# Which engine computes the low halves of the expert weights: VectorE and GpSimd by turns, or VectorE alone

## The chip, the cores and the metric

The kernel runs on one core of a Trainium2 chip. A core has TensorE (PE: matmuls, with its weight loads shown apart as PEld), VectorE (DVE), ScalarE (ACT), GpSimd (POOL) and SyncE (SP, which here issues the weight loads). The engines run side by side, each in its own order, and wait for one another through semaphores. The metric is the time of one execution in microseconds (us), as the median over several.

## The reference

Two blocks are run one after the other on 256 tokens of width 1024. The first has two layers of feed-forward, a convolution and recurrence mixer, and feed-forward again. The second has modulation, a recurrence beside an attention with selected keys, and at its end a mixture of 16 experts, the only part that the change touches:

```
y = zeros
for e in 16 experts:
    he = silu(hf @ w1[e]) * (hf @ w3[e])          # 1024 -> 512
    y = y + combine[:, e:e+1] * (he @ w2[e])      # 512 -> 1024
x = x + g2 * y
```

Each token has one group of four experts, and two experts within it; `combine` is zero for the others. All data are fp32.

## The kernel before, in words

**Weights in halves.** All weights lie in DRAM as blocks of 128 x 2048 numbers (1 MB), in the order of use. A block is two halves of 128 x 1024. A half has to be split before TensorE can use it: ScalarE writes its rounded copy (L197, type fp32r, the high half), and then VectorE or GpSimd subtracts that from the original (L202, the low half). A product is then three matmuls: high by high, weight low by input high, weight high by input low. For each weight half the experts do 6 matmuls of 512 columns.

**What sets the order.** `Weights.pump` issues the split of the next half: one cast on ScalarE, one subtraction on VectorE or GpSimd. It does so only while fewer than 6 halves (`NSPLIT`) are split or being split and not yet used up. `done` is called after the matmuls of a half: it frees that half's buffer, pumps one more, and lets background work take a step. So in the experts ScalarE and VectorE run some 6 halves ahead of TensorE, and each engine works strictly in the order written. SyncE loads blocks into 5 raw buffers, in the experts 2 more (`spare`); a raw buffer comes free when both of its halves are split.

**Which engine subtracts.** `W.gp` decides in L198: with 0 all subtractions go to VectorE, with n every n-th half goes to GpSimd. Elsewhere in the program it has the values 0, 1 and 2. Ahead of the experts it is 1 (five halves are split on GpSimd in advance); L1666 sets 3 for the experts.

**The experts.** The tokens of a group are gathered by a matmul with a 0/1 matrix (`gather`, L1511) and turned (`turn_gathered`, tile xg). For expert e, `up(e)` does 4 halves of w1 (m1) and 4 of w3 (m3) into the PSUM tile hp (L1536). VectorE then forms he (`weighted`, L1560). One expert later `turn(e)` transposes he on TensorE (L947), and VectorE and ScalarE split the result into ht (L317, L318). `down(e-1)` follows `up(e)`: 4 halves of w2 into y (L1594; for the last expert L1581). After each group `scatter` scales y (L1603), splits it (yh, L317, L318), multiplies it back to the tokens (L1612, L1613) and adds it to xres (L1614); its pieces are steps between the halves of the next but one expert. In the first expert a background job computes the routing weights in some 25 tiny VectorE instructions (L1458 to L1477), and `turn(0)` stands after the second half of w3 of expert 1.

Of the kernel before, what the change touches and what calls it, by code (L numbers as in the profile page):

```python
# [230 lines left out]
def kernel(ctx, tc, x, blocks, vecs, lnrows, consts, rows, bias_w, wr, out):  # L231
# [7 lines left out]
    W = Weights(tc, blocks, order, raw_pool, split_pool)  # L239
# [36 lines left out]
            soon.popleft()()  # L276
        step(M_WORK if work is None else work)

    # ---------------------------------------------------------------- start
    xres = apool.tile([128, 2, 1024], F32, name="xres")  # L280
    ident = cpool.tile([128, 128], F32, name="ident")
    vec = cpool.tile([128, NV], F32, name="vec")
# [96 lines left out]
    def new_xT():  # L379
        return apool.tile([128, 2, 8, 256], F32R, tag="xT", name="xT")  # L380
# [413 lines left out]
             lambda T, new: to_xT(xn, xres[:, T], T, new), xn, [("e1", l, 1, q) for q in range(4)])  # L794
        return xn

    # ------------------------------------------------------------ constants
    def setup():
        z = p1.tile([128, 6, 16], F32, name="sp")
        zv = [z[:, i] for i in range(6)]  # L800
        for l in range(2):
            nc.vector.tensor_scalar(z[:, 0, 8 * l:8 * l + 8], vec[:, l * V_LAYER + V_AP:l * V_LAYER + V_AP + 8],
                                    -1.0, None, op0=ALU.mult)
        nc.scalar.activation(zv[1], zv[0], AF.Abs)
        nc.scalar.activation(zv[1], zv[1], AF.Exp, scale=-1.0)
        nc.vector.tensor_scalar(zv[2], zv[1], 2.0, None, op0=ALU.add)
        nc.vector.reciprocal(zv[2], zv[2])
        nc.vector.tensor_mul(zv[1], zv[1], zv[2])
        nc.vector.tensor_mul(zv[2], zv[1], zv[1])
        n = 9  # L810
        nc.vector.tensor_scalar(zv[3], zv[2], 1.0 / (2 * n + 1), 1.0 / (2 * n - 1), op0=ALU.mult, op1=ALU.add)
        yield 0.6
        for k in range(n - 2, -1, -1):
            nc.vector.tensor_mul(zv[3], zv[3], zv[2])
            nc.vector.tensor_scalar(zv[3], zv[3], 1.0 / (2 * k + 1), None, op0=ALU.add)
        yield 1.2
        nc.vector.tensor_mul(zv[3], zv[3], zv[1])
        nc.vector.tensor_scalar(zv[0], zv[0], 0.0, None, op0=ALU.max)
        nc.vector.scalar_tensor_tensor(zv[3], zv[3], 2.0, zv[0], op0=ALU.mult, op1=ALU.add)
        for l in range(2):  # L820
            nc.vector.tensor_scalar(lruc[:, l, 0], z[:, 3, 8 * l:8 * l + 8], -8.0, None, op0=ALU.mult)
            nc.vector.tensor_scalar(lruc[:, l, 1], z[:, 3, 8 * l:8 * l + 8], 8.0, None, op0=ALU.mult)
        yield 0.5
# [44 lines left out]
                            ext_s[0:8, None, :].to_broadcast([8, 128, 512]))  # L868
        yield 0.1

    # ----------------------------------------------------------- the blocks
    xT = new_xT()
    to_xT(xT, xres[:, 0], 0, mid=lambda: W.pump(1))()
    W.pump(1)
# [9 lines left out]
                xT = ffn(l, part // 2, xT, l == 1 and part == 2)  # L884
    s1.close()

    # --------------------------------------------------------- second block
    s2 = ExitStack()
    p2 = s2.enter_context(tc.tile_pool(name="p2", bufs=1, reuse_waits="tile"))

# [442 lines left out]
    turn_[1] = True  # L1333
    s2.close()

    # ------------------------------------------------------- mixture of experts
    s3 = ExitStack()
    p3 = s3.enter_context(tc.tile_pool(name="p3", bufs=1, reuse_waits="tile"))
    g1b = p3.tile([128, 1024], F32, tag="yg", bufs=2, name="g1b")
# [323 lines left out]
    def early():  # L1663
        bg.append(weigh())

    W.gp = 3  # L1666
    experts(W, early, late)

    flag = nc.values_load(over[0:1, 0:1], min_val=0, max_val=1)
    with tc.If(flag > 0):  # L1670
# [4 lines left out]
        W = W2  # L1675
# [132 lines left out]
```

## Time and profile before

| | before |
|---|---|
| median of 3 runs (lowest to highest) | 1862.24 us (1861.23 to 1865.07) |
| span of the profiled execution | 1862.0 us |
| PE busy | 1755.7 us, 94% |
| DVE busy | 1328.0 us, 71% |
| ACT busy | 975.1 us, 52% |
| POOL busy | 547.4 us, 29% |
| L202 on DVE (raw) | 444 of 1510 ns, 663.1 us |
| L202 on POOL (raw) | 167 of 2655 ns, 442.1 us |

Busy time is an average over very different stages. The experts' matmuls start at 1528.3 us from the start of the span and end with it. In that stage the question is which engine the others wait for, so the stage has to be cut into stretches, and each read by itself. All positions below are us from the start of the span.

### The profile page before, as it was taken

The page shows a single profiled execution, that of the slowest core. Times are in us where ns is not written, and L with a number is a line of the kernel's source. Part 1 is how long each engine was busy: PE and PEld are TensorE (multiplying, and loading weights), DVE is VectorE, ACT ScalarE, POOL GpSimd, SP SyncE. Part 2 cuts the span into 40 slices and gives each one's busy share as a digit, 9 for nine tenths or more (in the row PEclk, how much of TensorE's full clock was granted, in tenths as well). Part 3 has the DMA queues.
Part 4 walks back from the last instruction along what each step waited for, and adds up shares of the span by engine and source line. Part 5 has one row for each costly group of instructions (what it writes and reads, how often), then busy time and mean ns, then how long its engine had stood idle before and what let it go on. Part 6 is the DMA issues. An engine that isn't in the chain of part 4 may idle for free. (4 is left out here: it accounts for less than half of the span.)

```text
span 1862.0 us, 27925 instructions
## 1 busy us (share of the span) xinstructions
PE 1755.7 (94%) x11369; PEld 1588.3 (85%) x11369; DVE 1328.0 (71%) x1569; ACT 975.1 (52%) x1340; POOL 547.4 (29%) x257
## 2 busy tenths in 40 slices
PE   8789999999999999999999999999798988999997
PEld 7789899999899989998989988999697666877775
DVE  6276778855756675668787466555878567899997
ACT  5254465654544444444756444444456456776773
POOL 0000144353200020003434441000546344555552
PEclk9989999999999999999999999999899889999999
DMA  7676554555556665765545646555333257978882
GB/s 291 170 261 253 219 181 159 182 205 180 216 203 241 248 246 181 255 242 204 182 159 186 211 147 243 190 181 181 129 113 108 108 230 268 348 283 335 302 315 115
DMA packets 57256, 394.26 MB, mean 212 GB/s; under 512 B 6912, under 2 KB 7216, under 8 KB 10912
## 3 DMA queue, kind: packets, MB, share of 16 engines
q1 hardware_dynamic: 52416, 375.94, 55.4%
q0 software_dynamic: 4128, 15.72, 3.0%
q8 instruction: 91, 1.49, 0.3%
q10 hardware_dynamic: 576, 0.74, 0.1%
q14 instruction: 45, 0.37, 0.1%
HBM read 389.20 MB, written 3.17 MB: 211 GB/s over the span
## 5 line engine op out<-in xcount | busy, mean ns | idle before, releaser
L202 DVE TENSOR_TENSOR split<-raw,split 128x1024 fp32r<-128x1024 f32 x444 | 663.1, 1510 | 293.1 <-ACT split L197 289.8
L202 POOL TENSOR_TENSOR split<-raw,split 128x1024 fp32r<-128x1024 f32 x167 | 442.1, 2655 | 1101.0 <-ACT split L197 1089.0
L197 ACT CAST split<-raw 128x1024 fp32r<-128x1024 f32 x611 | 628.4, 1048 | 256.1 <-PE mm L325 64.4
L323 PE MATMUL mmo<-xT,split 128*128 128x256 f32 x1248 | 354.0, 284 | 0.0
L324 PE MATMUL mmo<-xT,split 128*128 128x256 f32 x1248 | 353.7, 283 | 0.0
L325 PE MATMUL mmo<-xT,split 128*128 128x256 f32 x1248 | 353.6, 283 | 0.0
L325 PE MATMUL mm<-xT,split 128*128 128x256 f32 x968 | 274.2, 283 | 2.4 <-POOL split L202 2.4
L323 PE MATMUL mm<-xT,split 128*128 128x256 f32 x968 | 274.1, 283 | 0.0
L324 PE MATMUL mm<-xT,split 128*128 128x256 f32 x968 | 274.0, 283 | 0.0
L323 PEld LDWEIGHTS mmo<-xT,split 128*128 128x128 f32 x1248 | 239.4, 192 | 1.7
L324 PEld LDWEIGHTS mmo<-xT,split 128*128 128x128 f32 x1248 | 239.3, 192 | 1.7
L325 PEld LDWEIGHTS mmo<-xT,split 128*128 128x128 f32 x1248 | 239.3, 192 | 0.0
L376 PE MATMUL acc<-split,ht 128*128 128x512 f32 x816 | 200.6, 395 | 15.7 <-ACT split L197 15.5
L1536 PE MATMUL hp<-split,xg 128*128 128x512 f32 x768 | 190.6, 401 | 2.2 <-DVE split L202 1.4
L376 PEld LDWEIGHTS acc<-split,ht 128*128 128x128 f32 x816 | 150.3, 190 | 46.0 <-ACT split L197 15.7
L325 PEld LDWEIGHTS mm<-xT,split 128*128 128x128 f32 x968 | 185.3, 191 | 2.8 <-POOL split L202 2.8
L323 PEld LDWEIGHTS mm<-xT,split 128*128 128x128 f32 x968 | 185.3, 191 | 1.3
L324 PEld LDWEIGHTS mm<-xT,split 128*128 128x128 f32 x968 | 185.3, 191 | 1.3
L1536 PEld LDWEIGHTS hp<-split,xg 128*128 128x128 f32 x768 | 143.6, 190 | 38.3 <-DVE split L202 3.9
L1594 PE MATMUL y<-split,ht 128*128 128x512 f32 x360 | 89.8, 402 | 4.8 <-DVE ht L318 4.8
L1594 PEld LDWEIGHTS y<-split,ht 128*128 128x128 f32 x360 | 67.4, 190 | 22.8 <-DVE ht L318 7.4
L202 DVE TENSOR_TENSOR split<-spare,split 128x1024 fp32r<-128x1024 f32 x37 | 69.8, 1915 | 9.0 <-ACT split L197 9.0
(455 smaller groups left out, 2335.6 us busy)
## 6 DMA issues: line engine op xcount, KB each, us to landing
raw<-in_w_dram SPq DMA_DIRECT2D x328, 1024.0 KB, 4.9
spare<-in_w_dram SPq DMA_DIRECT2D x27, 1024.0 KB, 5.6
lng<-in_ln_dram POOLq DMA_DIRECT2D x6, 1024.0 KB, 4.9
raw<-in_w_dram SPq DMA_DIRECT2D x4, 512.0 KB, 7.6
scr<-ext_s POOLq DMA_DIRECT2D x1, 2048.0 KB, 47.4
cb<-in_row_dram POOLq DMA_DIRECT2D x3, 512.0 KB, 5.5
norm<-mrow POOLq DMA_DIRECT2D x2, 512.0 KB, 4.7
braw<-scr POOLq DMA_DIRECT2D x2, 512.0 KB, 4.8
```

The lines of the kernel that those rows point to most:

```text
L197: self.nc.scalar.copy(t[:, 0], r)
L202: eng.tensor_sub(t[:, 1], r, t[:, 0].bitcast(F32))
L323: nc.tensor.matmul(ps, w[:, 0, k], xT[:, 0, k], start=(k == 0), stop=False)
L324: nc.tensor.matmul(ps, w[:, 0, k], xT[:, 1, k], start=False, stop=False)
L325: nc.tensor.matmul(ps, w[:, 1, k], xT[:, 0, k], start=False, stop=(k == 7))
L376: nc.tensor.matmul(acc[T][n], a[:, hx], half[:, hw, n * 512:n * 512 + 512], start=(first and hx == 0 and hw == 0), stop=(last and hx == 1))
L1536: nc.tensor.matmul(ps, xgs[g][:, hx, k], wv[:, hw, kk], start=(k == 0 and hx == 0 and hw == 0), stop=(k == 7 and hx == 1))
L1594: nc.tensor.matmul(ys[g][n][:, 0:w], ht[:, hx, q], half[:, hw, o:o + w], start=(j == 0 and q == 0 and hx == 0 and hw == 0), stop=(j == 3 a ...
```

## The change

One number is changed: for the experts `W.gp` is 0 and no longer 3. Five comment lines are also made empty, which issues nothing and keeps the line numbers.

```
     def early():
         bg.append(weigh())

-    W.gp = 3
+    W.gp = 0
     experts(W, early, late)
```

On GpSimd's list, all that stood between the five subtractions ahead of the experts and the end goes. Before (h2s is the input of the experts, L1669 reads a flag after them):

```order
L1441 TENSOR_TENSOR h2s<-hh,h2s 128x1024
L202 TENSOR_TENSOR split<-raw,split 128x1024 x6
L202 TENSOR_TENSOR split<-spare,split 128x1024
L202 TENSOR_TENSOR split<-raw,split 128x1024 x4
...
L202 TENSOR_TENSOR split<-raw,split 128x1024 x4
L1669 TENSOR_LOAD over
```

And now:

```order
L1441 TENSOR_TENSOR h2s<-hh,h2s 128x1024
L202 TENSOR_TENSOR split<-raw,split 128x1024 x5
L1669 TENSOR_LOAD over
L1670 COMPARE_AND_BRANCH
```

62 subtractions leave GpSimd. The lists of TensorE and of ScalarE are the same as before.

On VectorE they stand where their halves come in the order. At the start of the experts, from the last routing numbers (cb) to the first he and ht, the list was:

```order
L1477 TENSOR_TENSOR cb<-rt 128x8
L202 TENSOR_TENSOR split<-spare,split 128x1024 x2
L202 TENSOR_TENSOR split<-raw,split 128x1024 x3
L1560 SCALAR_TENSOR_TENSOR he<-hp,cs,sl 128x512
L1488 TENSOR_REDUCE rt<-rank 128x1
L1489 TENSOR_SCALAR over<-rt 128x1
L1434 TENSOR_SCALAR Ps<-kc_14206,pos 128x128 x6
L202 TENSOR_TENSOR split<-raw,split 128x1024 x2
L318 TENSOR_TENSOR ht<-mm,ht 128x512
```

and is now:

```order
L1477 TENSOR_TENSOR cb<-rt 128x8
L202 TENSOR_TENSOR split<-spare,split 128x1024 x2
L202 TENSOR_TENSOR split<-raw,split 128x1024 x5
L1560 SCALAR_TENSOR_TENSOR he<-hp,cs,sl 128x512
L1488 TENSOR_REDUCE rt<-rank 128x1
L1489 TENSOR_SCALAR over<-rt 128x1
L1434 TENSOR_SCALAR Ps<-kc_14206,pos 128x128 x6
L202 TENSOR_TENSOR split<-raw,split 128x1024 x3
L318 TENSOR_TENSOR ht<-mm,ht 128x512
```

Ahead of the first he stand two subtractions more, and one more between it and the first ht.

Later, in the first scatter, VectorE's list between two he was this (ygs, yh and xres are the scatter's):

```order
L202 TENSOR_TENSOR split<-raw,split 128x1024 x4
L1603 TENSOR_TENSOR ygs<-y,g2b 128x512
L318 TENSOR_TENSOR yh<-ygs,yh 128x512
L1603 TENSOR_TENSOR ygs<-y,g2b 128x512
L318 TENSOR_TENSOR yh<-ygs,yh 128x512
L202 TENSOR_TENSOR split<-spare,split 128x1024 x2
L318 TENSOR_TENSOR ht<-mm,ht 128x512
L1614 TENSOR_TENSOR xres<-xres,acc 128x512
```

and is now:

```order
L202 TENSOR_TENSOR split<-raw,split 128x1024 x5
L1603 TENSOR_TENSOR ygs<-y,g2b 128x512
L318 TENSOR_TENSOR yh<-ygs,yh 128x512
L202 TENSOR_TENSOR split<-raw,split 128x1024
L1603 TENSOR_TENSOR ygs<-y,g2b 128x512
L318 TENSOR_TENSOR yh<-ygs,yh 128x512
L202 TENSOR_TENSOR split<-spare,split 128x1024 x2
L318 TENSOR_TENSOR ht<-mm,ht 128x512
L202 TENSOR_TENSOR split<-spare,split 128x1024
L1614 TENSOR_TENSOR xres<-xres,acc 128x512
```

One subtraction in three comes back, here also between the two pieces of the scatter.

## Rows read from the trace of the kernel before

**Rows 1.** Busy time by stretch: PE, PEld, DVE, ACT, POOL, clock, DMA share, GB/s.
```profile
1528.00:1563.50 35.50, 28.87 (x121) 22.48 (x121) 28.73 (x45) 22.54 (x29) 15.15 (x7) 0.90 0.67 240
1563.50:1617.00 53.50, 53.50 (x245) 43.42 (x244) 41.76 (x30) 41.49 (x47) 30.75 (x12) 1.00 0.91 336
1617.00:1639.20 22.20, 21.23 (x94) 16.80 (x93) 20.40 (x17) 15.87 (x18) 12.08 (x5) 1.00 0.85 315
1639.20:1719.40 80.20, 76.06 (x336) 59.55 (x335) 78.83 (x51) 57.28 (x64) 45.82 (x17) 1.00 0.85 314
1719.40:1797.70 78.30, 74.23 (x327) 58.06 (x326) 76.93 (x50) 55.82 (x63) 44.34 (x16) 1.00 0.85 313
1797.70:1845.90 48.20, 43.16 (x182) 33.48 (x182) 46.39 (x29) 30.57 (x32) 24.44 (x10) 0.96 0.51 194
```

**Rows 2.** Waits from 1528 to the end: total us, times, longest.
```profile
ACT split L197 <- PE hp L1536: 31.7, 83, 2.0
PE mm L947 <- DVE rt L1488: 5.1, 1, 5.1
PE y L1594 <- DVE ht L318: 4.8, 6, 1.1
```

**Rows 3.** Busy time of L202 alone: DVE, POOL, clock, DMA share, GB/s.
```profile
1528.00:1862.00 334.00, 247.21 (x125) 172.58 (x63) 0.98 0.76 280
60.00:200.00 140.00, 52.29 (x43) 0.00 (x0) 0.94 0.66 227
1639.20:1719.40 80.20, 67.10 (x32) 45.82 (x17) 1.00 0.85 314
```

**Rows 4.** Two subtractions at one time, in order of time: start, us, engine.
```profile
1535.80 2.42 POOL L202 TENSOR_TENSOR split<-spare,split 128x1024 fp32r<-128x1024 f32 x1 [1.96 <-ACT split L197]
1535.88 3.42 DVE L202 TENSOR_TENSOR split<-spare,split 128x1024 fp32r<-128x1024 f32 x1
```

**Rows 5.** TensorE in order of time, one expert and the end of a scatter.
```profile
1599.07 0.38 PE L1494 MATMUL mm<-ident,Ps 128*128 128x128 f32 x2
...
1599.66 5.86 PE L1594 MATMUL y<-split,ht 128*128 128x512 f32 x24
1605.35 5.77 PE L1536 MATMUL hp<-split,xg 128*128 128x512 f32 x24
1610.95 0.60 PE L947 MATMUL mm<-ident,he 128*128 128x128 f32 x4
1611.31 5.84 PE L1536 MATMUL hp<-split,xg 128*128 128x512 f32 x24
1616.99 1.33 PE L1594 MATMUL y<-split,ht 128*128 128x512 f32 x5
...
1717.06 0.40 PE L1612 MATMUL acc<-yh,PTs 128*128 128x512 f32 x1
...
1717.53 2.03 PE L1511 MATMUL mm<-h2s,Ps 128*128 128x512 f32 x8
1719.40 0.86 PE L1594 MATMUL y<-split,ht 128*128 128x512 f32 x3
```

**Rows 6.** The start of the experts, all engines in order of time.
```profile
1544.37 4.85 ACT L197 CAST split<-raw 128x1024 fp32r<-128x1024 f32 x5
...
1546.41 9.48 DVE L202 TENSOR_TENSOR split<-raw,split 128x1024 fp32r<-128x1024 f32 x3 [0.49 <-ACT split L197]
...
1555.82 0.74 DVE L1560 SCALAR_TENSOR_TENSOR he<-hp,cs,sl 128x512 f32<-128x512 f32 x1
...
1556.70 1.09 PE L947 MATMUL mm<-ident,he 128*128 128x128 f32 x4 [5.12 <-DVE rt L1488]
```

**Rows 7.** TensorE at the last expert.
```profile
1841.28 1.12 PE L947 MATMUL mm<-ident,he 128*128 128x128 f32 x4 [2.58 <-DVE he L1560]
...
1845.89 5.76 PE L1581 MATMUL y<-split,ht 128*128 128x512 f32 x24
```

**Rows 8.** Bytes moved, 1528 to the end in 40 equal slices.
```profile
GB/s 261 244 235 174 345 268 369 360 342 340 351 375 226 321 214 359 260 341 346 339 320 354 302 255 312 286 290 356 312 349 352 282 353 244 347 289 1 2 0 135
```

More of the change, by code (lines that the diff above doesn't have):

```diff
@@ L1664, in early @@
         bg.append(weigh())
-    W.gp = 3
+    W.gp = 0
     experts(W, early, late)
```

## Prediction

> **What bounds the kernel now.** I read the busy time of all engines cut into stretches of the expert stage first, since the page's shares mix stages. From 1563.5 to 1617 us TensorE is busy 53.50 of 53.50 us and VectorE 41.76: TensorE bounds, and VectorE has slack. From 1639.2 to 1797.7 it has turned round: VectorE is busy 78.83 of 80.20 and 76.93 of 78.30 us, TensorE some 4 us less than the stretch in each [rows 1]. Next I read the waits. ScalarE waits 83 times for TensorE to free a split buffer, so blocks have arrived in time; what stops TensorE comes from VectorE: the first transposes of he, ht before `down`, and the like [rows 2]. GpSimd holds nobody up by being late itself.
>
> Then I read the subtraction alone. From 60 to 200 us none runs on GpSimd, and 43 on VectorE take 52.29 us, 1.22 each. In the expert stage 125 take 247.21 us, 1.98 each [rows 3]. Two rows show how: GpSimd's starts at 1535.80 and takes 2.42 us; VectorE's starts 0.08 us later and takes 3.42, ending 1.08 us after GpSimd's [rows 4]. It made next to no progress beside it. So VectorE's excess is 247.21 - 125 x 1.22 = 94.7 us, over the 62 subtractions that this stage put on GpSimd 1.53 us each. Handing one to GpSimd costs VectorE more than the 1.22 us of doing it.
>
> **The change, part by part.** 62 subtractions leave GpSimd and join VectorE in the order of the halves. Bounds for what one costs VectorE in net: below, 1.22 - 1.53 = -0.31 us, if all of the excess goes with its cause; above, +1.98 us, if the mean of this stage stays what it is for all. I take the lower end, being the row of the only stretch here with GpSimd empty of them. VectorE then gets less to do.
>
> Take the group from 1639.2 to 1719.4, with 48 halves. VectorE's other work is 78.83 - 67.10 = 11.7 us [rows 1, 3]; with 48 x 1.22 = 58.6 us that is 70.3 instead of 78.8. TensorE needs more, so it is the bound. Its floor comes from stretches in which it did not wait [rows 5]. `down` of one expert to that of the next, with one turn of he: 1616.99 - 1599.66 = 17.33 us. A half: (1610.95 - 1605.35)/4 = 1.40. Four transposes: 0.36. `place_back`: 0.59. A piece of the scatter: 1717.53 - 1717.06 = 0.47, four 1.88. A gather: 1719.40 - 1717.53 = 1.87. A group is 4 x 17.33 + 2 x 0.36 (turning the gathered tokens) + 0.59 + 1.88 + 1.87 = 74.4 us. From there, stretch by stretch:
> - 1528 to 1563.5, the start. VectorE came free at 1546.41 - 0.49 = 1545.9 and took 9.48 us for three subtractions, then formed he at 1555.82 [rows 6]. Now five stand there: 1545.9 + 5 x 1.22 = 1552.0 (their casts end at 1549.2, so they do not bound). That is 3.8 us sooner, and TensorE, which idled 5.12 us before the transposes, goes on at 1552.9. From there to `down(0)` stand 0.36, two halves and a gather, 5.0 us, against 6.8 before at a mean granted clock of 0.90 in this stretch [rows 1]; so up to 5.6 us sooner. The third subtraction that now stands before the first ht may hold `down(0)` by some tenths. I take 5.0; bounds 3.8 (he alone) and 6.6 (all of TensorE's idle time there, 35.50 - 28.87).
> - 1563.5 to 1617: TensorE did not wait. Nothing.
> - 1617 to 1639.2: 17.33 + 1.88 + 1.87 = 21.1 against 22.2. 1.1 us.
> - 1639.2 to 1719.4: 74.4 against 80.2. 5.8 us.
> - 1719.4 to 1797.7: the last group needs no further gather, so 74.4 - 1.87 = 72.5 against 78.3. 5.8 us.
> - 1797.7 to 1845.9: two experts (34.66), then four halves and a turn of he (5.96), against 48.2. Of the 2.58 us for which TensorE waited for the last he [rows 7], some stays: behind the last half of `up(15)` the order puts a cast (1.0), a subtraction (1.22) and he (0.74), 3.0 us, and TensorE has two halves of cover, 2.8; I leave 0.5. 48.2 - 41.1 = 7.1 us.
> - 1845.9 to the end: no weights are left to split. Nothing.
>
> Sum 24.8 us. What is late next: in a scatter ScalarE's copy of ygs waits in order behind a subtraction and a multiplication on VectorE, and the casts queue behind that copy. With six buffers the casts fall back by most of their lead, so I take back 0.6 us for each of the three scatters, bounds 0 and 1.9, a third of the 5.8 us that a group loses to all waits now. Gain 23.0 us. The profiled execution took 1862.0 us, 0.2 below the median; on the median's scale the forecast is 1862.2 - 23.0 = 1839.2 us.
>
> A rule of the Trainium skill (Perfetto Trace Analysis, section Optimizing Scalar/DVE Operations) speaks against the change: where VectorE is saturated, work handed to ScalarE or even GpSimd may pay, though it warns that VectorE and GpSimd share an SBUF port and that moves between those two might not help. By its first half the move puts 62 x 1.22 = 76 us on a full engine. The trace has both the full engine [rows 1] and the lengthened subtraction [rows 4], and the second decides.
>
> **The rivals.** *Slower: the long subtractions are not GpSimd's doing.* If VectorE is lengthened by something that stays, such as weights landing at 313 to 336 GB/s, the mean stays 1.98 us. A group is then 48 x 1.98 + 11.7 = 106.7 us of VectorE, 26.5 above today's; over four groups that is 106 us, 1968 in all. The change loses as soon as the mean passes (80.2 - 11.7)/48 = 1.43 us. For it speaks only that the stretch with 1.22 moved 227 GB/s, less than here. Against it: from 1563.5 to 1617 the DMA share is at its highest, 0.91, and VectorE is least busy [rows 1]; and the end of the long subtraction keeps time with GpSimd's.
>
> *The feed becomes the bound.* A group is 24 blocks of 1.049 MB, 25.2 MB; in 74.4 us that is 338 GB/s, where the groups now get 314. If 314 is all that can be had, the groups stay, and only the start and the end gain, 12.1 us: 1850 us. Against it: slices of 8.35 us reach 369 and 375 GB/s [rows 8], the share is 0.85, and no wait for a block shows [rows 2]. The Trainium skill (SBUF, State Buffer, section Summary: rules for kernel authors) reckons with about 358 GB/s between HBM and SBUF. By that a group's blocks take an estimated 70 us and still fit, while an expert without a gather wants 6.29 MB in 17.33 us, 363 GB/s, and would live a little on the blocks held in advance; the slices above it make that no bound here.
>
> *Nothing to gain.* TensorE's waits stay and only change their names, since VectorE's order now holds more before each he and ht: within 0.2%, 1862. Against it stands that VectorE's total in a group falls from 78.8 to 70.3 us.
>
> **How the numbers follow.** Forecast 0.82 (its own range 1833 to 1847: the start's 6.6 and no scatter loss below; half of the groups' and the end's gain lost above). Feed 0.08, nothing 0.04, slower 0.06. About 0.2%, 3.7 us, is what a measurement of this kernel can tell from no change. Faster is the forecast and the feed, 0.90; same 0.04; slower 0.06. The range of 1833 to 1852 takes in the forecast's own and the feed's time.
>
> **What would show it.** In the changed profile L202 on VectorE has a mean near 1.22 us throughout the experts, 187 of them some 228 us in all; VectorE's busy share in the middle groups falls to about 95%, and TensorE's comes close to all. `down(0)` starts near 1558.5, and the periods of the groups are near 74.4 and 72.5. I am wrong if long subtractions stay although GpSimd is empty, if ScalarE's casts begin to wait for blocks, or if TensorE waits on at ht and yh.

## Result and the profile after

The changed kernel takes 1840.5 us (median of 4, 1835.7 to 1843.0) against 1862.8 (median of 4, 1861.2 to 1865.1): ratio 0.988, 95% interval 0.9865 to 0.9895. It is 22.2 us (1.2%) faster; forecast were 1839.2 us and 23.0 us.

The profiled execution has a span of 1833.9 us. It begins the experts' matmuls at 1522.2 us where the one before began at 1528.3, so 6.1 us of its difference lie ahead of the change, where both run the same instructions. From the first matmul of the experts to the end it is 333.7 us before and 311.7 after, 22.0 less. All stretches below are counted from such landmarks.

The busy time of the changed kernel by stretch stands against [rows 1], with the same columns and with its cuts at the same instructions:

```profile
1522.20:1551.40 29.20, 26.92 (x119) 20.79 (x119) 25.09 (x49) 22.45 (x28) 0.77 (x1) 1.00 0.76 278
1551.40:1604.70 53.30, 53.30 (x244) 43.23 (x243) 48.00 (x45) 41.36 (x46) 0.00 (x0) 1.00 0.93 354
1604.70:1627.10 22.40, 21.25 (x94) 16.69 (x93) 19.94 (x21) 15.74 (x18) 0.00 (x0) 1.00 0.80 297
1627.10:1702.80 75.70, 74.55 (x336) 59.94 (x335) 68.90 (x67) 57.09 (x64) 0.00 (x0) 1.00 0.90 334
1702.80:1776.60 73.80, 72.65 (x328) 58.42 (x327) 66.98 (x65) 56.20 (x63) 0.00 (x0) 1.00 0.89 333
1776.60:1817.60 41.00, 40.65 (x181) 32.62 (x180) 38.85 (x38) 29.93 (x32) 0.00 (x0) 1.00 0.58 218
```

In the two middle groups VectorE does 17 and 16 subtractions more and is busy for 68.90 and 66.98 us instead of 78.83 and 76.93. TensorE has the bound back: it lacks 1.15 us of each group, where it lacked 4.1.

The subtraction alone, busy time by engine and then shortest, median and longest of those from the raw buffers, answers to [rows 3]:

```profile
1528.00:1833.00 305.00, 223.10 (x185) 0.00 (x0) 0.99 0.81 302
```

```profile
L202 DVE TENSOR_TENSOR split<-raw,split x131: 1214/1224/1229, 1527.9 to 1812.3; 128x1024 fp32r<-128x1024 f32 x131
```

No long one is left: 185 take 223.10 us, where 125 took 247.21.

The start of the experts in order of time, VectorE and TensorE, answers to [rows 6]:

```profile
1538.77 5.76 DVE L202 TENSOR_TENSOR split<-raw,split 128x1024 fp32r<-128x1024 f32 x5
...
1544.45 0.74 DVE L1560 SCALAR_TENSOR_TENSOR he<-hp,cs,sl 128x512 f32<-128x512 f32 x1
...
1545.34 0.63 PE L947 MATMUL mm<-ident,he 128*128 128x128 f32 x4 [0.83 <-DVE rt L1488]
```

Five subtractions in 5.76 us, where three took 9.48. TensorE idles for 0.83 us ahead of the transposes instead of 5.12, and its granted clock in this stretch is 1.00, the upper level throughout, instead of a mean of 0.90. The last expert, answering to [rows 7]:

```profile
1814.36 0.63 PE L947 MATMUL mm<-ident,he 128*128 128x128 f32 x4 [0.35 <-DVE he L1560]
...
1817.63 5.76 PE L1581 MATMUL y<-split,ht 128*128 128x512 f32 x24
```

What TensorE still waits for is in the scatter. VectorE, ScalarE and TensorE in the first one, in order of time:

```profile
1614.83 0.62 ACT L317 CAST yh<-ygs 128x512 fp32r<-128x512 f32 x1 [1.90 <-DVE ygs L1603]
...
1618.30 0.62 ACT L317 CAST yh<-ygs 128x512 fp32r<-128x512 f32 x1 [1.90 <-DVE ygs L1603]
...
1622.18 0.69 DVE L318 TENSOR_TENSOR ht<-mm,ht 128x512 fp32r<-128x512 f32 x1
...
1623.92 0.68 DVE L1614 TENSOR_TENSOR xres<-xres,acc 128x512 f32<-128x512 f32 x1
...
1624.65 0.50 PE L1612 MATMUL acc<-yh,PTs 128*128 128x512 f32 x1 [1.15 <-DVE xres L1614]
```

ScalarE stands 1.90 us twice behind ygs. Its casts and its copy for ht come late by that, VectorE's ht and first xres come late behind them, and TensorE's fourth piece waits for the PSUM tile that this xres frees. The same 1.15 us come back in every scatter.

### The profile page after: what moved, and what is told of

Read it like the earlier page. It is cut to its first block, busy times and chain, and to the rows that moved or that the text cites. A ratio compares the mean times of both kernels' runs of the same rounds, so it can differ in the third digit from the quotient of the medians.

```text
span 1833.9 us, 27864 instructions
## 1 busy us (share of the span) xinstructions
PE 1738.9 (95%) x11369; PEld 1578.1 (86%) x11369; DVE 1304.2 (71%) x1631; ACT 975.0 (53%) x1340; POOL 376.9 (21%) x195
## 5 line engine op out<-in xcount | busy, mean ns | idle before, releaser
L202 DVE TENSOR_TENSOR split<-raw,split 128x1024 fp32r<-128x1024 f32 x489 | 645.2, 1332 | 298.9 <-ACT split L197 293.8
L202 POOL TENSOR_TENSOR split<-raw,split 128x1024 fp32r<-128x1024 f32 x122 | 317.6, 2613 | 992.3 <-ACT split L197 981.5
L553 DVE SCALAR_TENSOR_TENSOR junk<-raw,cb 128x1024 f32<-128x1024 f32 x48 | 58.5, 1219 | 23.2 <-ACT cb L551 23.2
```

Of the source, the lines that this page charges most:

```text
L202: eng.tensor_sub(t[:, 1], r, t[:, 0].bitcast(F32))
L553: nc.vector.scalar_tensor_tensor(junk, w, 1.0, cb, op0=ALU.mult, op1=ALU.mult, accum_out=modc[:, c:c + 1])
```

## Experiments

Each ran beside the kernel before on the same chip; ratios are to that, with the 95% interval.

**GpSimd repeats a third of the subtractions for nobody.**

```
             eng.tensor_sub(t[:, 1], r, t[:, 0].bitcast(F32))
+            if self.echo is not None and h % 3 == 0:
+                self.nc.gpsimd.tensor_sub(self.echo, r, t[:, 0].bitcast(F32))
...
+    W.echo = new_xT().rearrange("p h k t -> p (h k t)")[:, 0:1024]
```

> The changed kernel, with 62 subtractions more: for every third half of the experts GpSimd repeats VectorE's subtraction, from the same inputs, into a tile that nobody reads. VectorE's list is that of the changed kernel. Theory (a subtraction on GpSimd that reads SBUF holds up one on VectorE that has both inputs in SBUF): the 62 lengthen VectorE's by about 1.5 us each, 95 us in all; a group takes about 94 us of VectorE, about 20 more than now; some 1915 us (1890 to 1940), slower than the kernel before. Rival (what counts is which subtractions VectorE has to do and in which order, or the weights' landing lengthens them): VectorE's subtractions stay at 1.22 us, 1841 us (1838 to 1846).

1931.6 us, ratio 1.0378 (1.036 to 1.0395). In this kernel's trace (VectorE's is now L203) the subtractions on VectorE, as durations and as busy time, and then one group:

```profile
L203 DVE TENSOR_TENSOR split<-raw,split x132: 1208/1212/3455, 1527.9 to 1903.6; 128x1024 fp32r<-128x1024 f32 x132
```

```profile
1528.00:1910.00 382.00, 322.85 (x186) 0.00 (x0) 0.95 0.65 239
```

```profile
1664.50:1760.80 96.30, 80.60 (x335) 60.68 (x334) 94.68 (x68) 57.37 (x64) 46.78 (x16) 0.97 0.71 263
```

VectorE does the very work of the changed kernel. Its excess is 322.85 - 186 x 1.22 = 95.9 us, 1.55 us for each of the 62, where the trace of before gave 1.53. The longest took 3.455 us; in the kernel before it was 3.437. The weights land at 263 GB/s here, more slowly than in the changed kernel, and the long subtractions are back, on the same list of VectorE: the rivals that made the weights' landing or VectorE's own list their cause fall. VectorE is busy for 94.7 us in the group, against the 94 expected, and the group takes 96.3, with a granted clock of 0.97. The time lies in the expected range, 17 us above its middle.

**GpSimd kept busy, but only writing.**

```
+            if self.echo is not None and h % 3 == 0:
+                self.nc.gpsimd.memset(self.echo, 0.0)
+                self.nc.scalar.copy(self.probe, self.echo[:, 0:1])
             self.nc.scalar.copy(t[:, 0], r)
...
+    W.echo = new_xT().rearrange("p h k t -> p (h k t)")[:, 0:2816].bitcast(F32)
```

> The changed kernel, with GpSimd kept about as busy as before by work that only writes SBUF: for every third half it sets 128x2816 numbers to zero, about 2.6 us by the 954 ns of its 128x1024 memset, and a tiny copy on ScalarE (0.2 us) paces it. Theory that only GpSimd's reads collide with VectorE's second input: VectorE's subtractions stay at 1.22 us, and ScalarE's 62 small copies cost little, 1841 to 1848 us. Rival (any work of GpSimd on SBUF holds VectorE up): like the kernel with the repeated subtractions, about 1915 us.

1843.0 us, ratio 0.9903 (0.9886 to 0.9921). GpSimd's memsets and VectorE's subtractions (L206 here), shortest, median and longest:

```profile
L199 POOL MEMSET xT<- x62: 2447/2456/2577, 1524.1 to 1812.6; 128x2816 f32 x62
```

```profile
L206 DVE TENSOR_TENSOR split<-raw,split x132: 1208/1225/1228, 1527.8 to 1817.6; 128x1024 fp32r<-128x1024 f32 x132
```

62 instructions of 2.46 us on GpSimd, and not one subtraction on VectorE is longer than 1.23 us. The two did work at one time: in the group from 1632.0 to 1707.9 GpSimd was busy for 39.3 us and VectorE for 69.0. So it is not GpSimd's being busy that holds VectorE up. What its subtraction does and its memset does not is to read SBUF; no run here has GpSimd read SBUF beside VectorE with an instruction of another kind.

**Half of the change: every sixth half on GpSimd.**

```
-    W.gp = 0
+    W.gp = 6
```

> Half of the change: every sixth half of the experts on GpSimd, 31 instead of 62 or none. Theory (a subtraction on GpSimd costs VectorE 1.5 us and saves it 1.2, and the groups are bound by TensorE below 74 us of VectorE): a group has 40 x 1.22 + 8 x 1.53 + 11 = 72 us of VectorE, still under TensorE's 74, so most of the gain is there: 1845 us (1841 to 1851). Rival (the gain goes with the number moved): halfway, 1852 us.

1845.2 us, ratio 0.9912 (0.9894 to 0.9929); as expected, and not halfway. From the experts' first matmul to the end its trace has 312.4 us, against 311.7 with none on GpSimd and 333.7 before. The first matmuls of `down` for experts 4, 8 and 12 in its trace:

```profile
1636.50 5.76 PE L1594 MATMUL y<-split,ht 128*128 128x512 f32 x24
...
1711.90 5.76 PE L1594 MATMUL y<-split,ht 128*128 128x512 f32 x24
...
1785.44 5.76 PE L1594 MATMUL y<-split,ht 128*128 128x512 f32 x24
```

The groups take 75.4 and 73.5 us, as with none on GpSimd (75.7 and 73.8). In the first of them VectorE is busy for 69.1 us and TensorE for 75.1: while VectorE keeps below TensorE's time, what GpSimd costs it is hidden.

**The change from expert 12 on.**

```
         for e in range(16):
+            if e == 12 and W.gp == 3:
+                W.gp = 0
             up(e)
...
-    W.gp = 0
+    W.gp = 3
```

> The change from expert 12 on only: every third half on GpSimd before that, none after. Theory (the gain is a sum over stretches, each with its own backlog of VectorE): only the last stretch gains, 7 us, so about 1856 us (1853 to 1859). Rival (the gain is made at the start, where VectorE's backlog arises and is then carried along): no gain, 1862 us. Rival (a backlog at the end alone costs the 22 us): 1841 us.

1854.4 us, ratio 0.9959 (0.9945 to 0.9973). The gain is some 8.7 us; 7.1 of it are the last stretch, as in the whole change. The rest lies from `down(11)` to `down(12)`, with the last scatter, where its trace has 20.8 (1774.92 to 1795.68) instead of 22.8 us. The number changes ahead of `up(12)`, which stands before `down(11)`, and GpSimd's last subtraction starts at 1763.2 us. So the gain is a sum over stretches, and the last stretch inherits no backlog from those before.

Up to expert 12 this kernel issues what the kernel before issues, and yet its start takes 33.7 us (1528.5 to 1562.2) where that took 35.4: the three subtractions ahead of he took 7.28 us here and 9.48 there. Its next stretch, to `down(3)`, takes 54.8 us instead of 53.2, at a granted clock of 0.97 instead of 1.00. So neighbouring rows of two executions can differ by 1.5 us and more; the two together are 88.4 and 88.7.

**The changed kernel again, and three further edits.** The next four shared a chip and the runs of before (1861.3 us).

> The changed kernel once more, beside the three that follow, on one chip: 1841 us (1838 to 1844), 22 us below the kernel before. The profiled execution of the first comparison began its experts at 1522.2 us where the kernel before began at 1528.3, although nothing differs up to there. Theory: that is the spread of one execution, so here they begin anywhere from 1522 to 1531, and from the experts' first matmul to the end it is 312 us again (311 to 313). Rival: the change also shortens what stands ahead of the experts, and they begin at 1522 again.

1840.8 us, ratio 0.9895 (0.9879 to 0.9912). The experts begin at 1525.7 us and take 311.6 us to the end. Over all traces they began from 1522.2 to 1530.6, on either side of 1528.3 (leaving out the two whose code ahead of them differs): what stands ahead was not made shorter. What spreads it was not looked into.

**The scatter one step later.** ygs is scaled one step ahead of its split:

```
-            for n in range(2):
-                sl = slice(n * 512, n * 512 + 512)
-                nc.vector.tensor_mul(yg[:, sl], ys[g][n], g2b[:, sl])
-                split_out(yh[:, 0, sl], yh[:, 1, sl], yg[:, sl])
-                yield BIG
+            for n in range(3):
+                if n:
+                    sl = slice(n * 512 - 512, n * 512)
+                    split_out(yh[:, 0, sl], yh[:, 1, sl], yg[:, sl])
+                if n < 2:
+                    sl = slice(n * 512, n * 512 + 512)
+                    nc.vector.tensor_mul(yg[:, sl], ys[g][n], g2b[:, sl])
+                yield BIG
             yield BIG
-            yield BIG
```

> The changed kernel, with the scatter's scaling of y one step ahead of its split, so that ScalarE's copy finds ygs ready. Theory (the 1.15 us for which TensorE waits at the fourth piece of each scatter come from ScalarE waiting 1.9 us twice for ygs, which puts its casts, and by them ht and the first xres, behind): the wait goes, 1.3 us in each of three scatters, 3 to 4 us in all: 1837 us. Rival (the accumulator of the fourth piece waits for xres because VectorE's order has ht and a subtraction ahead of it, whatever ScalarE does): the wait stays, 1841 us.

1835.5 us, ratio 0.9861 (0.9845 to 0.9878). TensorE at the fourth piece, and `down` of experts 3, 4 and 8:

```profile
1630.61 0.40 PE L1614 MATMUL acc<-yh,PTs 128*128 128x512 f32 x1
1630.84 0.39 PE L1615 MATMUL acc<-yh,PTs 128*128 128x512 f32 x1
```

```profile
1611.97 5.76 PE L1594 MATMUL y<-split,ht 128*128 128x512 f32 x24
1632.94 5.77 PE L1594 MATMUL y<-split,ht 128*128 128x512 f32 x24
...
1707.17 5.76 PE L1594 MATMUL y<-split,ht 128*128 128x512 f32 x24
```

The wait is gone, although VectorE's list still has ht and a subtraction ahead of the first xres. 1632.94 - 1611.97 = 21.0 and 1707.17 - 1632.94 = 74.2 us: the floors of the prediction, 21.1 and 74.4. The wait came from ScalarE standing behind ygs, and its price is 1.4 us a scatter, 4.3 in all, a little more than the 3 to 4 expected.

**The routing without GpSimd.** The five subtractions ahead of the experts go to VectorE, behind the routing. With a list, `pump` issues the casts alone and notes the subtractions; `low` issues them on VectorE:

```
-        W.pump(NPRE)
+        W.pump(NPRE, early_)
         best_group()
...
-        W.pump(NPRE2)
+        W.low(early_)
+        W.pump(NPRE2, late_lows)
...
         turn_gathered(0)
+        W.low(late_lows)
+        late_lows.clear()
         W.pump(NSPLIT)
```

> The changed kernel, with the five subtractions ahead of the experts on VectorE too, behind the routing instead of beside it; the casts stay where they were. Theory (GpSimd's subtractions hold up any instruction of VectorE with two inputs in SBUF, however small): three instructions on 128x8 numbers in the choice of the group, which took 1.28, 2.26 and 2.06 us there, fall to about 0.17 us; the group's choice is done some 5 us sooner, and the experts begin 3 to 5 us sooner after the last matmuls of the routing's logits: 1836 us (1834 to 1839). Rival (those three are slow by themselves, for instance as the first after a change of shape): they stay slow, and the five subtractions on VectorE delay the experts, 1844 us.

1835.4 us, ratio 0.9869 (0.9853 to 0.9886). The choice of the group on VectorE, first in the changed kernel, then here, in order of time:

```profile
1509.11 1.28 DVE L1416 TENSOR_TENSOR rt<-rlg,rt 128x8 f32<-128x8 f32 x1
1510.42 2.26 DVE L1417 TENSOR_TENSOR rt<-rt,w 128x8 f32<-128x8 f32 x1
...
1512.72 0.17 DVE L1418 TENSOR_REDUCE rt<-rt 128x2 f32<-128x8 f32 x1
1512.92 2.06 DVE L1419 TENSOR_TENSOR goh<-w,rt 128x8 f32<-128x8 f32 x1
```

```profile
1511.60 0.17 DVE L1425 TENSOR_TENSOR rt<-rlg,rt 128x8 f32<-128x8 f32 x1
1511.80 0.17 DVE L1426 TENSOR_TENSOR rt<-rt,w 128x8 f32<-128x8 f32 x1
1512.00 0.16 DVE L1427 TENSOR_REDUCE rt<-rt 128x2 f32<-128x8 f32 x1
1512.20 0.17 DVE L1428 TENSOR_TENSOR goh<-w,rt 128x8 f32<-128x8 f32 x1
```

The three with two inputs in SBUF fall from 1.28, 2.26 and 2.06 to 0.17 us, and the reduction with one was never long. From the last matmul of the routing's logits to the experts' first it takes 8.2 us, where the changed kernel run again takes 13.4; 3 to 5 us less were expected. Some of it comes back: from the experts' first matmul to `down(0)` this kernel takes 30.9 us (1519.25 to 1550.16) instead of 29.2; TensorE waits 1.5 us for a cast there. The intervals of the two ratios just overlap (this one up to 0.9886, the changed kernel from 0.9879), so the gain rests on the traces.

**Both.**

> Both of these together. If the two waits are independent, their gains add: 1833 us (1829 to 1837). If one only moves the other's wait, the better of the two single times.

1835.1 us, ratio 0.9858 (0.9842 to 0.9875), the fastest median here. The sum of the two gains was expected, 1833, and the medians of the three cannot be told apart. In the traces, from the last matmul of the routing's logits to the end, the changed kernel run again takes 325.0 us, the first edit 320.1, the second 321.1 and both 317.8. Most of both gains is there, and the spread ahead of that point hides it.

## Why the prediction was right

By its own steps, in us, between the landmarks:

| stretch | forecast | measured |
|---|---|---|
| start, first matmul to `down(0)` | 5.0 | 35.4 - 29.2 = 6.2 |
| `down(0)` to `down(3)` | 0 | 53.2 - 53.3 = 0 |
| `down(3)` to `down(4)`, with a scatter | 1.1 | 22.2 - 22.4 = -0.2 |
| `down(4)` to `down(8)` | 5.8 | 80.2 - 75.7 = 4.5 |
| `down(8)` to `down(12)` | 5.8 | 78.3 - 73.8 = 4.5 |
| `down(12)` to `down(15)` | 7.1 | 48.2 - 41.1 = 7.1 |
| the end | 0 | 16.1 - 16.3 = -0.2 |
| three scatters, taken back | -1.8 | within the rows above |
| sum | 23.0 | 22.0 |

- The mechanism stands. Handing GpSimd a subtraction costs VectorE 1.53 us by the trace of before and 1.55 by the repeated ones, more than the 1.22 it saves. The lower end, -0.31 us net, was the right one to take.
- The floors were right: with the scatter's wait gone a group takes 74.2 us where 74.4 were worked out. VectorE's busy share in the groups fell further than forecast, to 91% and not 95%: the group kept the scatter's wait, and VectorE's other work shrank too (68.90 - 58.26 = 10.6 us and not 11.7), since yh was lengthened as the subtractions were.
- The term that was mis-sized is the scatter's: ScalarE's copy of ygs does put the casts behind, as forecast, but for 1.4 us a scatter and not 0.6. The prediction followed the casts and counted what the six buffers cover; it did not follow ht and xres, behind which the fourth piece waits for its PSUM tile.
- The start gained 6.2 and not 5.0, and its two parts were both off. Counted from the first matmul, he was formed 27.5 - 22.2 = 5.3 us sooner and not 3.8: the prediction held VectorE's time ahead of the five subtractions fixed, but the long subtraction of [rows 4] stood there and went as well (VectorE came to the five some 1.1 us sooner), and the five took 5.76 us, not 6.1. From the transposes to `down(0)` it then took 6.1 us, not 5.0; 0.69 of it TensorE waited for ScalarE's copy of the gathered tokens, and not for the subtraction ahead of ht. The granted clock did not fall.
- So the total is closer than its parts: 1.2 us forecast too little at the start and 2.1 too much in the three stretches with a scatter partly cancel. That the sum came within 1.0 us is partly luck. How the gain divides is not sharp either: against the kernel with the change from expert 12 on, the first row would be 33.7 - 29.2 = 4.5 and the second 54.8 - 53.3 = 1.5.
- The rivals: the feed did not bind, and of TensorE's waits in the groups only the scatter's is left. Over 53 us the weights landed at 354 GB/s, more than the 314 at which the groups stood before, and ScalarE's casts waited for TensorE. The slower rival falls by the first two experiments. As for the rule of the Trainium skill (Perfetto Trace Analysis, Optimizing Scalar/DVE Operations) that a saturated VectorE may be relieved by GpSimd, the trace takes the side of its warning: here the relief itself was what filled VectorE.

## What to carry to other kernels

Before work goes from VectorE to GpSimd, compare VectorE's mean with its shortest for the same instruction: where the mean is longer while GpSimd works, subtract the excess from what is relieved. An engine busy for all of a stretch need not have that much work. Instructions with two inputs in SBUF paid here, the smallest most in proportion, so a short chain that others wait for should not stand beside GpSimd's long ones.

## What was not expected of the hardware

Which of VectorE's instructions pay shows in the rows of the whole expert stage (total us, mean ns), first in the kernel before, then in the changed one:

```profile
L318 DVE TENSOR_TENSOR ht<-mm,ht 128x512 fp32r<-128x512 f32 x16 | 10.8, 678 | 0.0
L318 DVE TENSOR_TENSOR yh<-ygs,yh 128x512 fp32r<-128x512 f32 x6 | 8.0, 1328 | 4.1 <-ACT yh L317 4.1
```

```profile
L318 DVE TENSOR_TENSOR ht<-mm,ht 128x512 fp32r<-128x512 f32 x16 | 10.9, 684 | 0.0
L318 DVE TENSOR_TENSOR yh<-ygs,yh 128x512 fp32r<-128x512 f32 x6 | 4.2, 693 | 4.1 <-ACT yh L317 4.1
```

The same line and shape: with one input in PSUM (mm) it takes 678 ns in the kernel before, where GpSimd worked for over half of a group (45.82 of 80.20 us), and 684 after, and none of the 16 before took longer than 683; with both in SBUF (ygs, yh) 1328 and 693. The Trainium skill (SBUF — State Buffer, section Who interferes with whom) states both halves: two inputs in SBUF collide with GpSimd's reads, and not with an instruction of GpSimd that only writes. These rows and the memsets agree. And an instruction on 128x8 numbers can pay about as much as one on 128x1024: 2.26 us instead of 0.17, where the longest subtraction of before took 3.44 instead of 1.22.
